# Two-layer hybrid decoder trunk: the second layer's first scale and shift loaded and summed by halves, and ScalarE copies q and k in the first mixer

## The chip, the cores and the metric

The kernel runs as one program on one core of a Trainium2 chip. The metric is the device time of one execution in microseconds (us), from runs of the whole program. Of before there are three runs: 723.83 us is their median, 722.95 the lowest and 725.26 the highest. One further execution was profiled and took 724.93 us.

In what follows PE is TensorE, PEld its weight load, DVE is VectorE, ACT is ScalarE, POOL is GpSimd and SP is SyncE, which issues the DMAs of the weights. L12 is line 12 of the kernel.

## The reference

One sequence of 256 tokens with 1024 features goes through two layers. All is f32; the weights are some 265 MiB and each is used once, so that the program streams them from memory. Cut to what matters:

```python
cond = silu(c)                                  # one row of 1024
for l in range(2):
    mod = cond @ w_mod[l] + b_mod[l]            # w_mod[l]: 1024 x 6144
    sh1, sc1, g1, sh2, sc2, g2 = split(mod, 6)  # six rows of 1024 features
    h = layer_norm_plain(x) * (1 + sc1) + sh1
    q, k, v, p = split(h @ w_in[l], [512, 1024, 1536])
    a = attention(rope(q), rope(k), v)          # 8 heads of 64, causal
    m = pool_mixer(p, w_pool[l], pool_scale[l])
    x = layer_norm_affine(ALPHA * x + g1 * (concat(a, m) @ w_out[l]), ln1_g[l], ln1_b[l])
    h = layer_norm_plain(x) * (1 + sc2) + sh2
    y = grouped_moe(h)                          # 16 experts of 512, 2 per token
    x = layer_norm_affine(ALPHA * x + g2 * y, ln2_g[l], ln2_b[l])
```

The change is about sh1 and sc1 of the second layer (l = 1), which have to be complete before the second layer's h can be built, and about q and k of the first layer.

## The kernel before

**The stream.** All large weights pass through a ring of 1 MB tiles in SBUF, named wr. A Python class `Stream` (L56) holds them in one list, and SP issues their DMAs in that list's order: a tile is issued when the program frees a tile, as long as fewer than the allowed number (20) are live. A tile that is full therefore holds the stream up until PE or DVE has read it. The list for a layer is: the four quarters of w_in for q and k, p, v (two tiles each), the small w_pool, then the rows of w_mod for v = 2, 4, 3 (four tiles each; v counts sh1, sc1, g1, sh2, sc2, g2 as 0 to 5), w_out (four), v = 5 (four), and the eight pairs of experts. One pair is four tiles each of gate, up and down weights. Behind v = 5 of the first layer stand the four tiles of the second layer's v = 1, and behind the first layer's last expert the four of its v = 0; then come the second layer's q and k tiles. The first layer's own v = 0 and 1 are read in quarters of 256 features at the very start, between the q and k tiles.

**The work on them.** A row of mod is cond times 1024 x 1024 weights. PE does it in `mod_mm` (L297): 16 matmuls with cond as a stationary column, in four strips of the PE array that add up in one bank of PSUM. `mod_fin` copies that bank (ACT, L330), transposes it with four matmuls (L335), and DVE reduces it to 8 columns of 128 features and adds the bias (L337, L339). v = 5 ends in a row that is spread over all partitions. For v = 2, 4 and 3 DVE multiplies and adds the weights itself (`mod_dve`: L359 once and L361 seven times a row, one operation per 1024 x 128 weights), and PE closes the partial sums (L372, DVE L373 and L374).

**The mixer.** xn, the normalised x, is transposed by PE (L437, in `enter`), and DVE and ACT write it to hT with scale and shift (L442, L444). Then q and k of both token tiles are multiplied (L455), p (L504), rope is applied by DVE (L740 to L745), q and k are transposed again (L527), and copied to SBUF (L528: q by DVE, k by ACT); the scores follow (L534, L539), DVE's mask and row maximum on them (L554, L555), v (L578), the output (L622) and the norm. Then the router, and the experts: gate and up by L918, down by L960, with the norm of the next mixer at their end (L1104 to L1162).

**Order.** Each engine runs its instructions in the order in which the Python code issues them. `warm(n)` (L283) is a row of n matmuls on constants whose result nobody reads. In the first layer `mod_mm(l + 1, 1)` stands ahead of the norms and the router; in the second layer `warm(7)` stands at about the same place. `mod_fin(l + 1, 1)` is called in the first layer's second expert pair (pair 1 counted from 0).

Of the kernel before, what the change touches and what calls it, by code (L numbers as in the profile page):

```python
# [8 lines left out]
F = mybir.dt.float32  # L9
# [4 lines left out]
OP = mybir.AluOpType  # L14
AX = mybir.AxisListType

D = 1024
# [56 lines left out]
def tile_trunk(ctx, tc, x, c, w_mod, b_mod, w_in, w_pool, pool_scale, w_out, ln1_g, ln1_b,  # L74
# [30 lines left out]
    def add_mod01(h):  # L105

        w = w_mod[0].rearrange("(p k) n -> p k n", k=8)
        for v in (1, 0):
            st.add(("m01", h, v), w[:, :, v * D + h * 256:v * D + (h + 1) * 256])

    def add_qk(l, q):
        st.add(("in", l, "qk", q), w_in[l].rearrange("(k p) n -> p k n", p=128)[:, 2 * q:2 * q + 2, 0:D])

    def add_in(l):
        w = w_in[l].rearrange("(k p) n -> p k n", p=128)
        if l:
            for q in range(4):
                add_qk(l, q)
        for i, nm in ((3, "p"), (2, "v")):
            for q in range(2):  # L120
                st.add(("in", l, nm, q), w[:, 4 * q:4 * q + 4, i * 512:(i + 1) * 512])
# [35 lines left out]
    for l in range(DEPTH):  # L157
        add_in(l)
        st.add(("wp", l), lambda l=l: load_wp(l))
        for v in (2, 4, 3):  # L160
            add_mod(l, v)
        add_out(l)
        add_mod(l, 5)
        if l + 1 < DEPTH:
            add_mod(l + 1, 1)
        for i in range(NPAIR):
            add_pair(l, i)
        if l + 1 < DEPTH:
            add_mod(l + 1, 0)

# [77 lines left out]
    def bias_cols():  # L248
        b = ps()
        bv = b[:, 0:256].rearrange("p (m k r) -> p m k r", m=2, k=8)  # L250
        for k in range(8):
            T.transpose(bv[:, 0, k, 0:NV], brow[0:NV, k * 128:(k + 1) * 128], ident[0:NV, 0:NV])
            T.transpose(bv[:, 1, k, 0:NV], brow[0:NV, k::8], ident[0:NV, 0:NV])
        V.tensor_copy(bcol[:, :, :, 0:NV], bv[:, :, :, 0:NV])
        V.tensor_scalar(bcol[:, 0, :, 1], bcol[:, 0, :, 1], 1.0, None, op0=OP.add)

# [44 lines left out]

    col01 = const.tile([128, 2, 8], F, name="col01")
    colt[0, 0], colt[0, 1] = col01[:, 0], col01[:, 1]

# [14 lines left out]
    def mod01_fin(h, part):  # L319
        b = ps()  # L320
        for k in range(2):
            T.transpose(b[:, k * 128:(k + 1) * 128], part[:, k * 128:(k + 1) * 128], ident)
        o = col01[:, :, 2 * h:2 * h + 2]
        V.reduce_sum(o, b[:, 0:256].rearrange("p (k v o r) -> p v k o r", k=2, v=2, o=2)[:, :, :, :, 0], axis=AX.X)
        V.tensor_add(o, o, bcol[:, 0, 2 * h:2 * h + 2, 0:2].rearrange("p k v -> p v k"))

    def mod_fin(l, v):
# [102 lines left out]

    def enter(l, t, hT, xn):

        for h in range(2):
            b = ps()
            for k in range(4):
                kk = 4 * h + k
                T.transpose(b[:, k * 128:(k + 1) * 128], xn[:, t, kk * 128:(kk + 1) * 128], ident)  # L437
            for k in range(4):
                kk = 4 * h + k
                o, i = hT[:, kk, t * 128:(t + 1) * 128], b[:, k * 128:(k + 1) * 128]  # L440
                if h and t:
                    V.tensor_scalar(o, i, colt[l, 1][:, kk:kk + 1], colt[l, 0][:, kk:kk + 1], op0=OP.mult, op1=OP.add)  # L442
                else:
                    A.activation(o, i, AF.Identity, scale=colt[l, 1][:, kk:kk + 1], bias=colt[l, 0][:, kk:kk + 1])  # L444

    def mixer(l, hT, xn, ready):
        pq = [[ps(), ps()] for _ in range(2)]

        def qk_mm(t, qs=range(4), kks=range(2)):
            for q in qs:  # L450
                w = st.get(("in", l, "qk", q))
# [7 lines left out]

        if l:  # L460
            ready(0)
            qk_mm(0)
            ready(1)
        else:

# [10 lines left out]
        for t in range(2):  # L476
            if t:
                qk_mm(1, range(4) if l else (3,))
            A.activation(qk[:, t, 0:512], pq[t][0], AF.Copy, scale=DH ** -0.5)
# [43 lines left out]
        for t in range(2):  # L523
            for n, dst in ((0, qT), (1, kT)):
                b = ps()
                for cq in range(4):
                    T.transpose(b[:, cq * 128:(cq + 1) * 128], qk[:, t, n * 512 + cq * 128:n * 512 + (cq + 1) * 128], ident)  # L527
                (A.copy if n else V.tensor_copy)(dst[:, :, t * 128:(t + 1) * 128], b.rearrange("p (c s) -> p c s", c=4))  # L528

# [187 lines left out]
        gate = mod_fin(l, 5)  # L717
        if l + 1 < DEPTH:
            mod_mm(l + 1, 1)
        norms_of(1)  # L720
        exps(0)
        if l + 1 == DEPTH:
            warm(7)

# [116 lines left out]
    def experts(l, xh, xl, posm, rest):  # L841
# [230 lines left out]
        for i in range(NPAIR):  # L1072
# [19 lines left out]
            if i == 3:  # L1092
                gather(4)
            if i == 1 and l + 1 < DEPTH:
                mod_fin(l + 1, 1)
            if more:
# [27 lines left out]
    for l in range(DEPTH):  # L1124
# [19 lines left out]
        else:  # L1144
            mod_mm(l, 0)
            warm(3)
            own = []

            def ready(t):
                b = tiny.tile([128, 2, 6], F, name="bn")  # L1150
                if not t:
                    own.append(ends(0))
                for n in range(2):
# [4 lines left out]
                if not t:  # L1158
                    mod_fin(l, 0)
                    warm(8)  # L1160
                    own.append(ends(1))
                V.tensor_scalar(xn[:, t], xt[:, t], mv[:, 0:1], rs, op0=OP.subtract, op1=OP.mult)  # L1162
                enter(l, t, hT, xn)
        xh, xl, mes, gate = mixer(l, hT, xn, ready)
# [48 lines left out]
```

## Time and profile before

| | us |
|---|---|
| median of three runs (lowest, highest) | 723.83 (722.95, 725.26) |
| profiled execution | 724.93 |
| its span, first to last instruction | 723.1 |
| PE busy | 678.9 (94%) |
| DVE busy | 326.8 (45%) |
| ACT busy | 124.8 (17%) |
| DMA queue of SP: bytes, share of the 16 engines | 279.20 MB, 96.1% |

The span is 1.8 us short of the profiled execution's time. PE and the DMA queue are both busy nearly throughout: the page's slices show the DMA share at nine tenths or more except in four slices of the second layer (six or seven tenths), and in the last. By stages, the first mixer, norm and router end at 159.3 us, the first layer's experts run to 363.3, the second mixer, norm and router to 507.1, the second layer's experts to 709.5, and the last norm and the store of the output end the span.

In the rows of a window the engines stand in the order PE, PEld, DVE, ACT, POOL; a granted clock of 1.00 is TensorE's full 2.4 GHz and 0.50 its lower level of 1.2 GHz. In the rows of a timeline a group "x32" is 32 instructions; what stands in square brackets is the idle time of the engine just before the group and what ended it.

### The profile page before, as it was taken

Reading aid. Unit: us, or ns where it says so; the run is one execution under the profiler, and the core shown is the slowest. Engines: PE = TensorE matmul, PEld = TensorE weight load, DVE = VectorE, ACT = ScalarE, POOL = GpSimd, SP = SyncE. Lnnn points to the kernel's source line nnn. Section 1 sums busy time; section 2 is a strip of 40 time slices with the busy share of each in tenths; the row PEclk is TensorE's granted clock in tenths of the full one; section 3 lists DMA queues with packets and bytes.
Section 4 is the critical chain, followed back from the end, with each engine's and each line's share of the span. In section 5 each row is a group of like instructions: output and inputs, shape, how many; then the busy total and the mean of one; then the engine's idle time right before and its main releaser. Section 6 shows DMA issues by size and latency. Waiting matters only on the chain. (4 is left out here: it accounts for less than half of the span.)

```text
span 723.1 us, 8334 instructions
## 1 busy us (share of the span) xinstructions
PE 678.9 (94%) x3213; PEld 316.8 (44%) x3218; DVE 326.8 (45%) x582; ACT 124.8 (17%) x268; POOL 49.7 (7%) x76
## 2 busy tenths in 40 slices
PE   5999899999999999989979999998999999998994
PEld 2447555553333533423324575555333344342331
DVE  4008897662332532413153966666323243241305
ACT  1011432130110210121002035213210011012100
POOL 5001501100000000000010051010000000000002
PEclk9999999999999999999989999999999999999998
DMA  9999999999999999999999999767699999999992
GB/s 307 366 384 409 408 409 420 373 421 392 424 420 420 422 421 421 420 416 418 395 406 392 409 410 406 310 272 301 282 420 422 421 424 419 420 422 418 418 395 77
DMA packets 61729, 280.37 MB, mean 388 GB/s; under 512 B 5008, under 2 KB 14264, under 8 KB 38632
## 3 DMA queue, kind: packets, MB, share of 16 engines
q1 hardware_dynamic: 61040, 279.20, 96.1%
q8 instruction: 30, 0.49, 0.3%
q10 hardware_dynamic: 312, 0.32, 0.1%
q0 software_dynamic: 320, 0.14, 0.1%
q14 instruction: 27, 0.22, 0.1%
HBM read 278.59 MB, written 1.05 MB: 387 GB/s over the span
## 5 line engine op out<-in xcount | busy, mean ns | idle before, releaser
L918 PE MATMUL ps<-wr 128*64 128x512 f32 x1024 | 226.1, 596 | 0.0
L918 PEld LDWEIGHTS ps<-wr 128*64 128x64 f32 x1024 | 73.5, 138 | 147.2 <-issue 142.3
L960 PE MATMUL ps<-wr,s 128*64 128x512 f32 x512 | 113.8, 595 | 3.7 <-DVE s L945 2.9
L960 PEld LDWEIGHTS ps<-wr,s 128*64 128x64 f32 x512 | 35.5, 137 | 72.0 <-issue 63.8
L970 DVE SCALAR_TENSOR_TENSOR s<-ps,gc,gb 128x512 f32<-128x512 f32 x32 | 24.0, 748 | 84.0 <-PE ps L960 84.0
L455 PE MATMUL ps<-wr,hT 128*128 128x512 f32 x128 | 57.0, 597 | 0.4 <-ACT hT L429 0.2
L361 DVE SCALAR_TENSOR_TENSOR wr<-wr,condT 128x1024 f32<-128x1024 f32 x42 | 55.8, 1329 | 2.3 <-DMA wr<-in_w_mod_dram 0.9
L622 PE MATMUL ps<-wr,hT 128*128 128x512 f32 (+1 forms) x160 | 55.7, 507 | 0.1
L389 POOL TENSOR_TENSOR rs<-rs,mhalf 128x1 f32<-128x1 f32 x16 | 13.2, 823 | 554.1 <-DVE rs L388 554.1
L935 DVE TENSOR_TENSOR s<-s,ps 128x512 f32<-128x512 f32 x16 | 11.0, 687 | 86.5 <-PE ps L918 86.5
L973 ACT CAST wr<-s 128x512 fp32r<-128x512 f32 x30 | 18.5, 618 | 164.7 <-PE ps L918 107.7
L974 DVE TENSOR_TENSOR wr<-s,wr 128x512 fp32r<-128x512 f32 x30 | 20.8, 692 | 55.6 <-ACT wr L973 55.6
L622 PEld LDWEIGHTS ps<-wr,hT 128*128 128x128 f32 x160 | 30.2, 190 | 23.8 <-issue 21.5
L455 PEld LDWEIGHTS ps<-wr,hT 128*128 128x128 f32 x128 | 23.6, 190 | 28.9 <-issue 27.1
L984 PE MATMUL ps<-wr,sT 128*128 128x512 f32 x120 | 33.6, 413 | 0.0
L578 PE MATMUL ps<-wr,hT 128*128 128x512 f32 x64 | 28.3, 595 | 0.0
L504 PE MATMUL ps<-hT,wr 128*128 128x256 f32 x128 | 28.1, 380 | 0.0
L984 PEld LDWEIGHTS ps<-wr,sT 128*128 128x128 f32 x120 | 20.9, 189 | 16.3 <-issue 13.0
L933 DVE SCALAR_TENSOR_TENSOR s<-s,ps 128x512 f32<-128x512 f32 x16 | 11.0, 685 | 36.7 <-ACT s L932 36.7
L504 PEld LDWEIGHTS ps<-hT,wr 128*128 128x128 f32 x128 | 24.2, 190 | 4.5 <-issue 1.3
L876 PE MATMUL ps<-s,xn 128*128 128x512 f32 x64 | 25.4, 398 | 0.3 <-DVE s L854 0.3
L996 DVE TENSOR_TENSOR xt<-xt,ps 128x512 f32<-128x512 f32 x40 | 25.2, 683 | 0.5
(240 smaller groups left out, 611.5 us busy)
## 6 DMA issues: line engine op xcount, KB each, us to landing
wr<-in_w_gate_dram SPq DMA_DIRECT2D x64, 1024.0 KB, 19.3
wr<-in_w_up_dram SPq DMA_DIRECT2D x60, 1024.0 KB, 19.3
wr<-in_w_down_dram SPq DMA_DIRECT2D x56, 1024.0 KB, 19.5
wr<-in_w_mod_dram SPq DMA_DIRECT2D x48, 1024.0 KB, 15.1
wr<-in_w_in_dram SPq DMA_DIRECT2D x16, 1024.0 KB, 15.1
wr<-in_w_out_dram SPq DMA_DIRECT2D x8, 1024.0 KB, 18.7
wr<-in_w_down_dram SPq DMA_DIRECT2D x12, 512.0 KB, 11.1
wr<-in_w_up_dram SPq DMA_DIRECT2D x8, 512.0 KB, 17.4
```

Source lines behind the costliest of these rows:

```text
L361: V.scalar_tensor_tensor(acc, w[:, kk], condT[:, k, 0:1], acc, op0=OP.mult, op1=OP.add)
L455: T.matmul(pq[t][n], hT[:, k, t * 128:(t + 1) * 128], w[:, kk, n * 512:(n + 1) * 512], start=(k == 0), stop=(k == 7))
L504: T.matmul(pp[g // 2][:, (g % 2) * 256:(g % 2) * 256 + 256], w[:, kk, g * 128:(g + 1) * 128], hT[:, k, :], start=(k == 0 and g % 2 == 0), ...
L578: T.matmul(pv[t], hT[:, k, t * 128:(t + 1) * 128], w[:, kk, :], start=(k == 0), stop=(k == 7))
L622: T.matmul(py[t][-1][:, 0:c1 - c0], catT[:, k, t * 128:(t + 1) * 128], w[:, kk, n * 512 + c0:n * 512 + c1], start=(q == 2 and kk == 0), st ...
L876: T.matmul(b, xs[:, t, k * 128:(k + 1) * 128], SX[i][t], start=(n == 0), stop=(n == 3))
L918: T.matmul(bs[nm][64 * j:64 * j + 64, :], XE[i][k // 4][:, k % 4, c0:c0 + 64], st.get((nm, l, 2 * i + j, q))[:, k - k0, :], start=(k == 0) ...
L960: T.matmul(bo[n][64 * j:64 * j + 64, :], AT[i][:, k, 64 * j:64 * j + 64], st.get(("d", l, 2 * i + j, q))[:, k - k0, (n - n0) * 512:(n - n0 ...
L970: V.scalar_tensor_tensor(o, bo[n], GC[i], g2[:, c0], op0=OP.mult, op1=OP.mult)
L974: V.tensor_sub(ol[:, c0], o, oh[:, c0].bitcast(F))
L984: T.matmul(b, STt[i][:, t * 128:(t + 1) * 128], o[:, n * 512:(n + 1) * 512], start=(start and j == 0), stop=(stop and j == 1), skip_group_ ...
L996: V.tensor_add(b if i == NPAIR - 3 else xt[:, t, c0], xt[:, t, c0], b)
```

## The change

The first layer's stream loses the four tiles of v = 1 ahead of the experts. Behind the first layer's last expert, v = 1 and v = 0 of the second layer are now read by halves of 512 features: four tiles of 128 x 4 x 512 for features 0 to 511 (v = 1 and 0, two halves of the rows each), two of q and k's quarters, four tiles for features 512 to 1023, and the other two quarters. Each half is summed by PE in `mod1`: 16 matmuls, one copy by ACT, and closed in `mod1_fin` by four transposes, one reduction for scale and shift together and one addition of the biases. The 1 that is added to the scale is now in the bias columns (L252 to L255 before).

The second mixer's opening is written out anew: transposes of token tile 0's first half, q and k of token tile 0 from the first two quarters, the second half's `mod1`, then token tile 1, and so on. The normalised xn is written in two halves of 512. In the first layer `warm(7)` now stands where `mod_mm(l + 1, 1)` was, as in the second. In the first mixer ACT makes all four copies of L528 (now L573), of which DVE made two.

In the lines below h is the half, v the row of mod, q the quarter or the half of the rows.

```diff
+    def add_mod1(h):
+        w = w_mod[1].rearrange("(p k) n -> p k n", k=8)
+        for v in (1, 0):
+            for q in range(2):
+                st.add(("m1", h, v, q), w[:, 4 * q:4 * q + 4, v * D + h * 512:v * D + (h + 1) * 512])
     def add_qk(l, q):
...
         w = w_in[l].rearrange("(k p) n -> p k n", p=128)
-        if l:
-            for q in range(4):
-                add_qk(l, q)
         for i, nm in ((3, "p"), (2, "v")):
...
         add_mod(l, 5)
-        if l + 1 < DEPTH:
-            add_mod(l + 1, 1)
         for i in range(NPAIR):
...
         if l + 1 < DEPTH:
-            add_mod(l + 1, 0)
+            for q in range(4):
+                if q % 2 == 0:
+                    add_mod1(q // 2)
+                add_qk(l + 1, q)
...
         V.tensor_copy(bcol[:, :, :, 0:NV], bv[:, :, :, 0:NV])
-        V.tensor_scalar(bcol[:, 0, :, 1], bcol[:, 0, :, 1], 1.0, None, op0=OP.add)
+        V.tensor_scalar(bcol[:, 0, :, 1:8:6], bcol[:, 0, :, 1:8:6], 1.0, None, op0=OP.add)
...
         V.tensor_add(o, o, bcol[:, 0, 2 * h:2 * h + 2, 0:2].rearrange("p k v -> p v k"))
+    def mod1(h):
+        acc = ps()
+        for k in range(8):
+            for v in range(2):
+                j = 2 * v + k % 2
+                T.matmul(acc[32 * j:32 * j + 32, :], condT[:, k, :], st.get(("m1", h, v, k // 4))[:, k % 4, :],
+                         start=(k < 2), stop=(k > 5))
+            if k % 4 == 3:
+                for v in range(2):
+                    st.free(("m1", h, v, k // 4))
+        part = s2()
+        A.copy(part, acc)
+        return part
+    def mod1_fin(h, part):
+        b = ps()
+        for k in range(4):
+            T.transpose(b[:, k * 128:(k + 1) * 128], part[:, k * 128:(k + 1) * 128], ident)
+        o = col01[:, 1, :, 4 * h:4 * h + 4]
+        V.reduce_sum(o, b.rearrange("p (k v o r) -> p v k o r", k=4, v=2, o=2)[:, :, :, :, 0], axis=AX.X)
+        V.tensor_add(o, o, bcol[:, 0, 4 * h:4 * h + 4, 6:8].rearrange("p k v -> p v k"))
...
-    def enter(l, t, hT, xn):
-        for h in range(2):
-            b = ps()
-            for k in range(4):
-                kk = 4 * h + k
-                T.transpose(b[:, k * 128:(k + 1) * 128], xn[:, t, kk * 128:(kk + 1) * 128], ident)
+    def enter(l, t, h, hT, xn):
+        b = ps()
+        for k in range(4):
+            kk = 4 * h + k
+            T.transpose(b[:, k * 128:(k + 1) * 128], xn[:, t, kk * 128:(kk + 1) * 128], ident)
+        def fin():
             for k in range(4):
...
                     A.activation(o, i, AF.Identity, scale=colt[l, 1][:, kk:kk + 1], bias=colt[l, 0][:, kk:kk + 1])
+        return fin
     def mixer(l, hT, xn, ready):
-        pq = [[ps(), ps()] for _ in range(2)]
+        pq = [[], []]
         def qk_mm(t, qs=range(4), kks=range(2)):
+            if not pq[t]:
+                pq[t] += ps(), ps()
             for q in qs:
...
         if l:
             ready(0)
-            qk_mm(0)
+            enter(l, 0, 0, hT, xn)()
+            qk_mm(0, (0, 1))
+            part = mod1(1)
             ready(1)
+            enter(l, 1, 0, hT, xn)()
+            mod1_fin(1, part)
+            fins = [enter(l, 0, 1, hT, xn)]
+            qk_mm(1, (0, 1))
+            fins.append(enter(l, 1, 1, hT, xn))
+            for fin in fins:
+                fin()
+            qk_mm(0, (2, 3))
         else:
...
             if t:
-                qk_mm(1, range(4) if l else (3,))
+                qk_mm(1, (2, 3) if l else (3,))
             A.activation(qk[:, t, 0:512], pq[t][0], AF.Copy, scale=DH ** -0.5)
...
                     T.transpose(b[:, cq * 128:(cq + 1) * 128], qk[:, t, n * 512 + cq * 128:n * 512 + (cq + 1) * 128], ident)
-                (A.copy if n else V.tensor_copy)(dst[:, :, t * 128:(t + 1) * 128], b.rearrange("p (c s) -> p c s", c=4))
+                (A.copy if n or not l else V.tensor_copy)(dst[:, :, t * 128:(t + 1) * 128], b.rearrange("p (c s) -> p c s", c=4))
...
         gate = mod_fin(l, 5)
-        if l + 1 < DEPTH:
-            mod_mm(l + 1, 1)
         norms_of(1)
         exps(0)
-        if l + 1 == DEPTH:
-            warm(7)
+        warm(7)
...
                 gather(4)
-            if i == 1 and l + 1 < DEPTH:
-                mod_fin(l + 1, 1)
             if more:
...
         else:
-            mod_mm(l, 0)
+            part0 = mod1(0)
             warm(3)
...
                 b = tiny.tile([128, 2, 6], F, name="bn")
-                if not t:
-                    own.append(ends(0))
+                own.append(ends(t))
                 for n in range(2):
...
                 if not t:
-                    mod_fin(l, 0)
+                    mod1_fin(0, part0)
                     warm(8)
-                    own.append(ends(1))
-                V.tensor_scalar(xn[:, t], xt[:, t], mv[:, 0:1], rs, op0=OP.subtract, op1=OP.mult)
-                enter(l, t, hT, xn)
+                for n in range(2):
+                    V.tensor_scalar(xn[:, t, n * 512:(n + 1) * 512], xt[:, t, n * 512:(n + 1) * 512],
+                                    mv[:, 0:1], rs, op0=OP.subtract, op1=OP.mult)
         xh, xl, mes, gate = mixer(l, hT, xn, ready)
```

The order of the instructions at three places follows. First SP's DMAs ahead of the first layer's experts, before and after (mod is w_mod; a row is a run of DMAs of one shape):

```order
L146 DMA wp<-in_w_pool_dram 128x4x128
L56 DMA wr<-in_w_mod_dram 128x2x1024 x12
L56 DMA wr<-in_w_out_dram 128x2x1024 x4
L56 DMA wr<-in_w_mod_dram 128x2x1024 x8
L56 DMA wr<-in_w_gate_dram 128x2048 x4
```

```order
L150 DMA wp<-in_w_pool_dram 128x4x128
L56 DMA wr<-in_w_mod_dram 128x2x1024 x12
L56 DMA wr<-in_w_out_dram 128x2x1024 x4
L56 DMA wr<-in_w_mod_dram 128x2x1024 x4
L56 DMA wr<-in_w_gate_dram 128x2048 x4
```

The twelve tiles for v = 2, 4, 3 and w_out stay; of the eight tiles for v = 5 and the second layer's v = 1, four remain.

Next SP's DMAs from the first layer's last down weights on, before and after:

```order
L56 DMA wr<-in_w_down_dram 128x2x512 x6
L56 DMA wr<-in_w_down_dram 128x512 x4
L56 DMA wr<-in_w_mod_dram 128x2x1024 x4
L56 DMA wr<-in_w_in_dram 128x2x1024 x4
L56 DMA wr<-in_w_in_dram 128x4x512 x4
L146 DMA wp<-in_w_pool_dram 128x4x128
```

```order
L56 DMA wr<-in_w_down_dram 128x2x512 x6
L56 DMA wr<-in_w_down_dram 128x512 x4
L56 DMA wr<-in_w_mod_dram 128x4x512 x4
L56 DMA wr<-in_w_in_dram 128x2x1024 x2
L56 DMA wr<-in_w_mod_dram 128x4x512 x4
L56 DMA wr<-in_w_in_dram 128x2x1024 x2
L56 DMA wr<-in_w_in_dram 128x4x512 x4
L150 DMA wp<-in_w_pool_dram 128x4x128
```

Four tiles of 2 rows x 1024 have become two groups of four tiles of 4 rows x 512, the second one between the second and the third quarter of q and k.

Last, PE at the opening of the second mixer, from the last row of `warm` to p, before and after (col names are left out by the view; L437 and L466 are the transposes into hT, L455 and L489 q and k, L340 `mod1`, L352 its transposes, L504 and L549 p):

```order
L283 MATMUL ps<-ones 128x512
L437 MATMUL ps<-ident,xn 128x128 x8
L455 MATMUL ps<-wr,hT 128x512 x16
L437 MATMUL ps<-ident,xn 128x128 x8
L455 MATMUL ps<-wr,hT 128x512 x16
L504 MATMUL ps<-hT,wr 128x256 x32
```

```order
L288 MATMUL ps<-ones 128x512
L466 MATMUL ps<-ident,xn 128x128 x4
L489 MATMUL ps<-wr,hT 128x512 x8
L340 MATMUL ps<-wr,condT 32x512 x16
L466 MATMUL ps<-ident,xn 128x128 x4
L352 MATMUL ps<-ident,s_5813 128x128 x4
L466 MATMUL ps<-ident,xn 128x128 x4
L489 MATMUL ps<-wr,hT 128x512 x8
L466 MATMUL ps<-ident,xn 128x128 x4
L489 MATMUL ps<-wr,hT 128x512 x16
L549 MATMUL ps<-hT,wr 128x256 x32
```

Before, PE ran both token tiles' q and k one after the other, each after eight transposes. Now the second half's `mod1` and its transposes stand after the first eight matmuls of q and k, and all that follows stands behind them.

## Rows read from the trace of the kernel before

**Rows 1.** Both layers' experts: length, busy us (instructions) by engine, clock, DMA share, GB/s

```profile
159.34:363.32 203.98, 198.07 (x914) 77.28 (x913) 64.85 (x116) 25.74 (x42) 0.00 (x0) 0.99 1.01 415
507.08:709.47 202.39, 197.18 (x910) 76.81 (x909) 64.49 (x114) 25.26 (x41) 0.00 (x0) 1.00 0.97 400
```

**Rows 2.** The page's 40 slices: TensorE's granted clock in tenths, GB/s of the DMAs

```profile
PEclk9999999999999999999989999999999999999998
...
GB/s 307 366 384 409 408 409 420 373 421 392 424 420 420 422 421 421 420 416 418 395 406 392 409 410 406 310 272 301 282 420 422 421 424 419 420 422 418 418 395 77
```

**Rows 3.** Waits of SP, window 140 to 170: us in total, times, longest

```profile
SPq L56 <- PE ps L918: 20.2, 3, 15.0
```

**Rows 4.** Waits of SP, window 484 to 520

```profile
SPq L56 <- PE ps L918: 22.6, 3, 17.4
```

**Rows 5.** DMA issued at 163.0 to 163.2: KB, us to landing

```profile
wr<-in_w_up_dram SPq DMA_DIRECT2D x1, 1024.0 KB, 5.8
```

**Rows 6.** DMA issued at 510.7 to 510.9

```profile
wr<-in_w_up_dram SPq DMA_DIRECT2D x1, 1024.0 KB, 5.0
```

**Rows 7.** Last expert DMA of the first layer, issued at 353.4

```profile
wr<-in_w_down_dram SPq DMA_DIRECT2D x1, 256.0 KB, 8.0
```

**Rows 8.** Timeline of DVE in the first mixer: start, us, operation, idle before and releaser

```profile
63.05 10.82 DVE L361 SCALAR_TENSOR_TENSOR wr<-wr,condT 128x1024 f32<-128x1024 f32 x7
73.79 1.27 DVE L528 COPY wr<-ps 128x512 f32<-128x512 f32 x2
76.77 0.70 DVE L554 TENSOR_TENSOR ps<-ps,mask 128x512 f32<-128x512 f32 x1 [1.70 <-PE ps L534]
...
88.54 9.21 DVE L361 SCALAR_TENSOR_TENSOR wr<-wr,condT 128x1024 f32<-128x1024 f32 x7
```

**Rows 9.** Timeline of ACT in the first mixer

```profile
69.42 1.07 ACT L513 COPY wr<-ps 128x512 f32<-128x512 f32 x2 [14.45 <-PE ps L504]
```

**Rows 10.** Timeline of DVE ahead of the first layer's experts

```profile
140.54 1.23 DVE L646 TENSOR_SCALAR wr<-xt,mv,rs 128x1024 f32<-128x1024 f32 x1 [0.73 <-POOL rs L389]
```

**Rows 11.** Timeline of PE: first mixer, router, pair 1, boundary, second mixer

```profile
74.62 2.08 PE L534 MATMUL ps<-wr 64*128 64x128 f32 x16 [3.48 <-DVE wr L528]
...
135.54 7.05 PE L297 MATMUL ps<-wr,condT 128*32 128x512 f32 x64
...
200.35 0.66 PE L335 MATMUL ps<-ident,s 128*128 128x128 f32 x4 [1.22 <-ACT s L330]
...
372.74 1.93 PE L297 MATMUL ps<-wr,condT 128*32 128x512 f32 x8 [2.49 <-DMA wr<-in_w_mod_dram]
...
380.43 1.98 PE L455 MATMUL ps<-wr,hT 128*128 128x512 f32 x4
...
409.25 13.98 PE L504 MATMUL ps<-hT,wr 128*128 128x256 f32 x64
...
428.36 1.16 PE L534 MATMUL ps<-wr 64*128 64x128 f32 x16 [0.35 <-DVE wr L528]
...
488.04 1.67 PE L283 MATMUL ps<-ones 128*128 128x512 bf16 x7
```

**Rows 12.** Windows: the loads of p and v, then those of w_mod in the second layer

```profile
382.91:393.79 10.88, 10.88 (x26) 4.75 (x25) 1.78 (x4) 0.00 (x0) 0.55 (x1) 1.00 1.05 386
394.65:415.10 20.45, 20.34 (x66) 11.75 (x65) 17.96 (x18) 3.65 (x8) 0.15 (x1) 1.00 1.03 409
```

**Rows 13.** Last DMAs for v = 4 of the second layer, issued at 396.3

```profile
wr<-in_w_mod_dram SPq DMA_DIRECT2D x2, 1024.0 KB, 18.7
```

**Rows 14.** Timeline of DVE in the second mixer

```profile
410.09 7.89 DVE L361 SCALAR_TENSOR_TENSOR wr<-wr,condT 128x1024 f32<-128x1024 f32 x6 [0.37 <-DMA wr<-in_w_mod_dram]
...
420.37 0.29 DVE L745 TENSOR_TENSOR xn<-s 128x128 f32<-128x128 f32 x1
425.86 1.29 DVE L373 TENSOR_REDUCE col<-ps 128x4 f32<-128x512 f32 x2 [5.20 <-PE ps L372]
```

**Rows 15.** A window with the clock at its lower level

```profile
74.61:78.03 3.42, 3.41 (x24) 3.26 (x26) 1.69 (x3) 0.00 (x0) 3.18 (x6) 0.50 1.04 413
```

More of the change, by code (lines that the diff above doesn't have):

```diff
@@ L300, in mod_mm @@
         macc[l, v] = acc
-    col01 = const.tile([128, 2, 8], F, name="col01")
-    colt[0, 0], colt[0, 1] = col01[:, 0], col01[:, 1]
+    col01 = const.tile([128, DEPTH, 2, 8], F, name="col01")
+    for l in range(DEPTH):
+        for v in range(2):
+            colt[l, v] = col01[:, l, v]
     def mod01(h):
@@ L322, in mod01_fin @@
             T.transpose(b[:, k * 128:(k + 1) * 128], part[:, k * 128:(k + 1) * 128], ident)
-        o = col01[:, :, 2 * h:2 * h + 2]
+        o = col01[:, 0, :, 2 * h:2 * h + 2]
         V.reduce_sum(o, b[:, 0:256].rearrange("p (k v o r) -> p v k o r", k=2, v=2, o=2)[:, :, :, :, 0], axis=AX.X)
         V.tensor_add(o, o, bcol[:, 0, 2 * h:2 * h + 2, 0:2].rearrange("p k v -> p v k"))
+    def mod1(h):
[6 more added lines that the diff above has]
+            if k % 4 == 3:
+                for v in range(2):
+                    st.free(("m1", h, v, k // 4))
[9 more added lines that the diff above has]
+        V.tensor_add(o, o, bcol[:, 0, 4 * h:4 * h + 4, 6:8].rearrange("p k v -> p v k"))
     def mod_fin(l, v):
```

## The prediction

> **What bounds the kernel now.** I read the windows by stage first. In both layers' experts PE and the DMA queue are full together: PE is busy 198.1 of 204.0 us and 197.2 of 202.4 us, and the DMAs move 415 and 400 GB/s [rows 1]. So the end follows the start of the second layer's experts by a fixed 202.4 us and a tail, and what the change gains in the first layer counts only if it is still there at 507.1.
>
> Next the waits of SP and single DMAs, to see which of the two sets the length of the first layer's experts. When these start, 19 expert tiles are in the ring, and SP stands 15.0 us at the next one until PE frees a gate tile [rows 3]; in the second layer the same wait is 17.4 us [rows 4]. This 20th tile lands 5.8 us after its issue at 163.1, thus at 168.9, some 0.8 us later behind its issue than in the second layer (5.0), where the queue had run dry [rows 5, 6]. The layer's last expert piece lands at 353.4 + 8.0 = 361.4 [rows 7]. Between lie 192.5 us. The layer has 96 expert tiles (16 experts, three matrices of 2 MB); 96 - 19 = 77, so a tile takes 2.50 us, which is 420 GB/s, as the slices there show, nearly all 420 to 424 [rows 2]: the queue has no pause. The first layer's experts are therefore bound by DMA from the 20th tile on, and by nothing else that the change touches.
>
> Then the timelines, for what stands ahead of the 20th tile and behind the last piece.
>
> **First mixer: ACT copies q.** DVE's seven L361 end at 63.05 + 10.82 = 73.87, and only then can it copy q (1.27 us for two); the mask waits further for the scores and starts at 76.77 [rows 8]. ACT is free at 69.42 + 1.07 = 70.49, and makes a copy of that size in 0.54 [rows 9]; four end at about 72.7, so PE's scores, now at 74.62 after 3.48 idle [rows 11], can start near 71.5 and the mask right at 73.87. DVE gains 76.77 - 73.87 = 2.9. Its next seven L361 (88.54, 9.21, without a pause) [rows 8] come that much earlier, and the mixer waits for them: -2.9. Bounds: nothing, if another engine holds the mixer, and -3.5, PE's whole idle time.
>
> **Ahead of the experts: `mod_mm` out, `warm(7)` in.** PE's 64 L297 run from 135.54 to 142.59 [rows 11], half of them this row's (3.5 us), while DVE has the normalised rows at 140.54 + 1.23 = 141.77 [rows 10]. PE was late by 0.8; without the 32 it is at 139.1, with `warm` (1.67 us, row at 488.04) [rows 11] at 140.7, and DVE is last: -0.8. The experts start 3.7 earlier.
>
> **The ring takes the head start.** Four tiles (10 us of stream) fewer stand ahead of the experts. But the ring holds no more than before: the queue runs dry at the 19th tile and waits for PE, as it does in the second layer. So the 20th tile is issued 3.7 earlier and lands 5.0 instead of 5.8 after it: 4.5 earlier, and so does the last expert piece, at 356.9. The 4 MB that the stream had carried early are now behind it. From the other side: if the queue did not run dry, they would come 10 us earlier.
>
> **Pair 1: `mod_fin` out.** PE's pause of 1.22 and 0.66 of transposes at 200.35 [rows 11] go. Nothing comes of it where DMA sets the end; I count 0 (bound -1.9).
>
> **Behind the last expert.** Before, v = 0 (4 tiles) is complete at about 372.7 and q and k start at 380.43, 7.7 later [rows 11]. Now the first half's four tiles have runs of 2 KB per partition row, as p and v have; those load at 386 GB/s, 2.72 us a tile, and the rows of w_mod with 4 KB runs at 409, 2.56 [rows 12]. I take 2.72 (bounds 2.50, a tile of the experts, and 2.87, by the 366 GB/s of the second slice [rows 2], in which rows of w_mod with 1 KB runs are loaded). The half lands at 356.9 + 10.9 = 367.8. Of the 7.7 I take off up to 1.4 (four transposes instead of eight, half a norm): q and k at 374 to 375.5. Half of a token tile's q and k takes a quarter of 409.25 - 380.43 = 28.8 [rows 11], 7.2; the second half lands at 367.8 + 5.1 + 10.9 = 383.8, so PE waits 1 to 2.5 us. One us of `mod1`, about 2 for copy, transposes and hT, and 21.6 of q and k put p at 408 to 410, where it was: PE keeps nothing of the 4.5.
>
> **The second mixer's v = 4.** This is the step that decides. Before, the last tile of v = 4 lands at 396.3 + 18.7 = 415.0 [rows 13], 53.6 behind the last expert piece. Now there are eight tiles for four: 53.6 - 4 x 2.56 + 8 x 2.72 = 65.1, so it lands at 356.9 + 65.1 = 422.0, 7.0 later. Behind it DVE has two more L361 and rope, and then idles 5.20 until PE is through with p and the transposes (425.86) [rows 14]. 7.0 - 5.2 = 1.8: DVE is late now, by that much, and the copies, the scores and the whole second half of the mixer follow. From there to 507.1 the DMAs fall to 272 to 310 GB/s [rows 2], so they don't bound it, and the experts start 1.8 later.
>
> **Sum.** -2.9 (first mixer), -0.8 (`mod_mm`) and -0.8 (the dry queue) make -4.5 at the last expert piece. The stream behind it is 8 x 2.72 - 4 x 2.56 = 11.5 longer, and DVE had 5.2 to spare: -4.5 + 11.5 - 5.2 = +1.8. Against the profiled execution, 724.93, that is 726.7; the median of the runs lies 1.1 lower, at 723.83, so I forecast 725.6.
>
> **A rule on short runs.** The loads with 2 KB runs go at 386 GB/s, against 409 for 4 KB [rows 12]. The Trainium skill, "DMA: Bandwidth & Descriptors", Specifications, gives 512 B as the least transfer for line rate; by it the eight tiles would go at the experts' speed. That would be a rival: in rows, eight tiles at 2.50, 8 x 0.22 = 1.8 less, no change, 723.8. The row of p and v speaks against it; for it only that four tiles are a short sample.
>
> **The rivals.** *The gain stays (faster).* If the mixer opens so much better that DVE's v = 4 is not last, or the stream keeps its lead, PE's path counts: 3.7 and 1.9 from pair 1 less about 1.6 for the new wait, -4.0, thus 719.8. For it speaks the PE work taken out ahead of the experts; against it the 15.0 us at a full ring [rows 3]. *The clock falls (slower).* PE's wait of 3.48 at 74.62 was followed by 3.42 us at 0.50 [rows 15], in which the 16 L534 took 2.08 instead of 1.16 [rows 11]. Now PE has new waits: 1 to 2.5 us for the second half near 383, and about 1.5 ahead of the scores near 429, where it had 0.35 [rows 11]. If the clock falls there, half of 3.42 is lost on PE: +1.7 once, 727.3, and +3.4 twice, 729. It decides where a new wait is nearer to 3.48 than to 0.35, which left the later L534 at full speed. The Trainium skill, "TensorE: Matmul & The Clock Gate", Part 1, has the clock fall after idling, and this trace agrees with its 0.50 behind the wait. *The first mixer gains nothing (slower).* If DVE's later work, or PE's, holds the first mixer where it was, the 2.9 are missing at v = 4: +4.7, 728.5.
>
> **How the numbers follow.** Forecast 0.44 (724 to 727); the short runs are free 0.12 (723.8); the gain stays 0.22 (719.8 to 721.5); the clock falls 0.14 (727.3 to 729); no gain in the first mixer 0.08 (728.5). About 0.3% (2.2 us) is what a measurement of this kernel can tell from no change: faster is below 721.7, slower above 726.0. Faster takes the third case, 0.22. Slower takes the last two and a third of the forecast's, 0.14 + 0.08 + 0.15 = 0.37. Same has the rest, 0.41. The range from 720.3 to 728.2 leaves out about half of the third case and half of the last two.
>
> **What would show it.** In the profile after: the first mixer's mask right behind L391 near 73.9 and no low clock there; the experts' start near 155.6; the DMAs dry for some 10 us ahead of it; the first layer's last expert landing near 356.9; p starting within 2 us of 409; DVE with no idle time between rope and the reduction (L403), which starts near 427.7; the second layer's experts near 508.9. I am wrong if v = 4 lands before 420, if the queue does not run dry ahead of the first layer's experts, or if something between the reduction and the router takes up the delay.

## The result: 1.6% slower, and the profile after

The changed kernel takes 735.88 us (median of 4 runs, 734.74 to 737.44) against 724.24 of before (now four runs): a ratio of 1.0163 (95% interval 1.0135 to 1.0192), 11.6 us more where I had forecast 1.8. The profiled execution is the slowest of the four, 737.44, with a span of 735.6.

Up to the first layer's last expert things went as drawn, only smaller. The slices of the DMAs' rate first:

```profile
GB/s 306 365 385 409 409 414 420 387 172 422 421 420 419 420 420 418 419 414 410 387 395 390 409 409 409 312 257 368 216 419 421 419 419 421 418 419 416 417 396 80
```

The ninth slice, ahead of the experts, fell from 421 in [rows 2] to 172 GB/s: the queue ran dry, from the landing of the 19th expert tile at 154.9 to the issue of the next at 162.1. SP's wait there is now as long as the second layer's was [rows 3, 4]:

```profile
SPq L56 <- PE ps L960: 22.6, 3, 17.4
```

Of the DMAs, the 20th expert tile (issued at 162.1), the last expert piece (351.96) and the last two tiles of v = 4 (the later one at 406.3), with KB and us to landing:

```profile
wr<-in_w_up_dram SPq DMA_DIRECT2D x1, 1024.0 KB, 5.2
...
wr<-in_w_down_dram SPq DMA_DIRECT2D x1, 256.0 KB, 8.1
...
wr<-in_w_mod_dram SPq DMA_DIRECT2D x2, 1024.0 KB, 18.8
```

The last expert piece lands at 360.0, 1.4 earlier than before and not 4.5 [rows 7]; v = 4 lands at 425.1, 10.0 later than before [rows 13]. Between them are 65.1 us, the number that I had worked out: the tiles' rate was right, the head start was not.

DVE in the first mixer (start, us, operation), as in [rows 8]:

```profile
63.91 10.82 DVE L391 SCALAR_TENSOR_TENSOR wr<-wr,condT 128x1024 f32<-128x1024 f32 x7
74.66 0.69 DVE L599 TENSOR_TENSOR ps<-ps,mask 128x512 f32<-128x512 f32 x1
...
87.07 9.21 DVE L391 SCALAR_TENSOR_TENSOR wr<-wr,condT 128x1024 f32<-128x1024 f32 x7
```

ACT's copies let the mask follow L391 without a pause, at 74.66. But this execution had begun 0.9 us late (p at 56.17, before at 55.31; the thirteen profiles of this document have it anywhere from 55.24 to 57.68), and the next seven L391 start only 1.5 earlier than before.

PE: first the second mixer's v in the kernel before, which [rows 11] don't show; then, after, from the first mixer's transposes of v = 4 to the second mixer's v:

```profile
431.19 7.13 PE L578 MATMUL ps<-wr,hT 128*128 128x512 f32 x16
```

```profile
96.43 1.45 PE L402 MATMUL ps<-ident,wr 128*128 128x128 f32 x8 [2.38 <-DVE wr L391]
97.81 1.98 PE L646 MATMUL ps<-wr 128*64 128x128 f32 x16
...
412.43 13.98 PE L549 MATMUL ps<-hT,wr 128*128 128x256 f32 x64
...
433.32 1.94 PE L572 MATMUL ps<-ident,xn 128*128 128x128 f32 x8 [3.88 <-DVE xn L787]
...
438.25 2.08 PE L579 MATMUL ps<-wr 64*128 64x128 f32 x16
...
442.79 7.13 PE L623 MATMUL ps<-wr,hT 128*128 128x512 f32 x16
```

PE now waits 2.38 for v = 4 at 96.43, and there is the low clock behind it; p of the second mixer starts at 412.43, 3.2 later than before; and ahead of the transposes of q and k PE waits 3.88. The low clock in two windows:

```profile
97.07:100.48 3.41, 3.41 (x23) 2.26 (x22) 3.19 (x5) 0.59 (x1) 1.06 (x1) 0.50 1.03 412
431.58:441.82 10.24, 7.40 (x40) 6.37 (x42) 8.18 (x18) 1.17 (x2) 8.04 (x15) 0.50 1.02 410
```

DVE in the second mixer, from v = 4 through rope to the reduction, which answers to [rows 14]:

```profile
420.07 7.89 DVE L391 SCALAR_TENSOR_TENSOR wr<-wr,condT 128x1024 f32<-128x1024 f32 x6 [0.32 <-DMA wr<-in_w_mod_dram]
427.88 2.08 DVE L782 TENSOR_TENSOR s<-xn,cs 128x128 f32<-128x128 f32 x1
429.88 0.28 DVE L783 TENSOR_TENSOR s<-xn,cs 128x128 f32<-128x128 f32 x1
430.08 1.61 DVE L784 TENSOR_TENSOR s<-xn,cs 128x128 f32<-128x128 f32 x1
431.62 0.28 DVE L785 TENSOR_TENSOR s<-xn,cs 128x128 f32<-128x128 f32 x1
431.93 1.05 DVE L786 TENSOR_TENSOR xn<-s 128x128 f32<-128x128 f32 x1
432.90 0.28 DVE L787 TENSOR_TENSOR xn<-s 128x128 f32<-128x128 f32 x1
433.10 0.82 DVE L782 TENSOR_TENSOR s<-xn,cs 128x128 f32<-128x128 f32 x1
433.85 0.30 DVE L783 TENSOR_TENSOR s<-xn,cs 128x128 f32<-128x128 f32 x1
434.07 0.47 DVE L784 TENSOR_TENSOR s<-xn,cs 128x128 f32<-128x128 f32 x1
434.46 0.28 DVE L785 TENSOR_TENSOR s<-xn,cs 128x128 f32<-128x128 f32 x1
434.77 0.70 DVE L786 TENSOR_TENSOR xn<-s 128x128 f32<-128x128 f32 x1
435.40 0.30 DVE L787 TENSOR_TENSOR xn<-s 128x128 f32<-128x128 f32 x1
435.62 1.27 DVE L403 TENSOR_REDUCE col<-ps 128x4 f32<-128x512 f32 x2
```

Here is what I had not seen at all. Rope starts 10.0 late, by as much as v = 4 lands late, and then its twelve operations, 0.28 us each before, take 7.8 us together instead of 2.8 (427.88 to 435.70, before 417.90 to 420.66): six of them take 0.47 to 2.08. POOL in the same stretch does the pooling of p. Its first operation before, then its operations after:

```profile
423.99 1.99 POOL L749 TENSOR_TENSOR wr<-wr 128x1084 f32<-128x1084 f32 x1 [13.91 <-ACT wr L513]
```

```profile
427.16 2.65 POOL L791 TENSOR_TENSOR wr<-wr 128x1084 f32<-128x1084 f32 x1 [8.64 <-DMA wr<-in_w_mod_dram]
429.89 1.66 POOL L792 TENSOR_TENSOR wr<-wr 128x807 f32<-128x807 f32 x1
431.63 1.20 POOL L793 TENSOR_TENSOR wr<-wr 128x530 f32<-128x530 f32 x1
432.91 0.86 POOL L794 TENSOR_TENSOR wr<-wr 128x256 f32<-128x256 f32 x1
```

Each slow operation of DVE ends just behind one of POOL's: 427.88 + 2.08 = 429.96 behind 427.16 + 2.65 = 429.81; 431.69 behind 431.55; 432.98 behind 432.83; 433.92 behind 433.77. The last two, at 434.07 and 434.77, end in the same way behind two shorter operations of POOL's. Before, rope was over at 420.7 and POOL began at 424. The reduction behind it, L403, reads PSUM and takes 1.27 beside POOL, before 1.29.

In the profiled executions the second layer's experts start 11.6 late, at 518.7 against 507.1. These are: 1.4 saved up to the last expert piece; 11.4 of stream added; 5.2 of DVE's slack used up; 5.0 for rope beside POOL; and about 1.8 from the reduction (9.8 late) to v on PE (442.79 against 431.19, 11.6 late), with the clock at 0.50. -1.4 + 11.4 - 5.2 + 5.0 + 1.8 = 11.6. The two spans are 12.5 apart; the other 0.9 arises behind that start. That the medians of the runs are 11.6 apart too is chance.

### The profile page after: what moved, and what is told of

Its sections match the earlier page's. It is cut to its first block, busy times and chain, and to the rows that moved or that the text cites. A ratio compares the mean times of both kernels' runs of the same rounds, so it can differ in the third digit from the quotient of the medians.

```text
span 735.6 us, 8361 instructions
## 1 busy us (share of the span) xinstructions
PE 688.3 (94%) x3225; PEld 321.8 (44%) x3225; DVE 331.2 (45%) x582; ACT 126.2 (17%) x270; POOL 50.9 (7%) x76
## 5 line engine op out<-in xcount | busy, mean ns | idle before, releaser
L489 PE MATMUL ps<-wr,hT 128*128 128x512 f32 x128 | 57.1, 596 | 0.5 <-ACT hT L475 0.5
L391 DVE SCALAR_TENSOR_TENSOR wr<-wr,condT 128x1024 f32<-128x1024 f32 x42 | 55.8, 1329 | 2.3 <-DMA wr<-in_w_mod_dram 0.9
L489 PEld LDWEIGHTS ps<-wr,hT 128*128 128x128 f32 x128 | 23.5, 190 | 28.3 <-issue 26.8
L549 PE MATMUL ps<-hT,wr 128*128 128x256 f32 x128 | 28.1, 380 | 0.0
L549 PEld LDWEIGHTS ps<-hT,wr 128*128 128x128 f32 x128 | 24.2, 190 | 4.5 <-issue 1.0
## 6 DMA issues: line engine op xcount, KB each, us to landing
wr<-in_w_down_dram SPq DMA_DIRECT2D x12, 512.0 KB, 11.6
```

Source lines behind the costliest of these rows:

```text
L391: V.scalar_tensor_tensor(acc, w[:, kk], condT[:, k, 0:1], acc, op0=OP.mult, op1=OP.add)
L489: T.matmul(pq[t][n], hT[:, k, t * 128:(t + 1) * 128], w[:, kk, n * 512:(n + 1) * 512], start=(k == 0), stop=(k == 7))
L549: T.matmul(pp[g // 2][:, (g % 2) * 256:(g % 2) * 256 + 256], w[:, kk, g * 128:(g + 1) * 128], hT[:, k, :], start=(k == 0 and g % 2 == 0), ...
```

## The experiments

Each ratio is to the runs of the kernel before that stand beside that run on record. Their medians differ (723.0 to 724.5 us), so rows are compared by their ratios. Microseconds won or lost are worked out from these ratios at 724 us, and positions from the one profiled execution of each run.

| run | median us (runs) | ratio to before (95% interval) |
|---|---|---|
| the change | 735.9 (4) | 1.0163 (1.0135, 1.0192) |
| e1: POOL waits for rope | 730.2 (4) | 1.0087 (1.0053, 1.0120) |
| e2: PE's wait ahead of q, k filled | 735.1 (4) | 1.0165 (1.0136, 1.0193) |
| e4: change, DVE copies q | 738.8 (4) | 1.0209 (1.0181, 1.0238) |
| e7: change, v behind v = 4 | 728.0 (10) | 1.0059 (1.0041, 1.0078) |
| e8: e7 and filled wait in first mixer | 727.6 (12) | 1.0042 (1.0026, 1.0058) |
| e3: before, DVE delayed 6.6 us | 731.9 (4) | 1.0113 (1.0085, 1.0142) |
| e11: e3, POOL waits for rope | 727.8 (10) | 1.0050 (1.0030, 1.0070) |
| e9: before, the move alone | 733.2 (4) | 1.0119 (1.0088, 1.0151) |
| e5: before, ACT copies alone | 721.8 (12) | 0.9971 (0.9954, 0.9987) |
| e6: e5 and filled wait | 721.1 (12) | 0.9953 (0.9933, 0.9974) |
| e10: e6 and filled wait at the boundary | 721.8 (12) | 0.9966 (0.9951, 0.9982) |

**e1: POOL held until rope is through** (from the changed kernel).

```diff
+        if l:
+            P.tensor_copy(tiny.tile([128, 1], F, name="hold", bufs=1), qk[:, 1, 8:9])
         pr = pool(pz, SA, SB)
```

> The changed kernel, with one small copy on POOL that reads the last of rope's output ahead of the second mixer's pooling, so that POOL starts when DVE is through with rope. Theory (POOL's pooling, running beside it, slows rope from 2.8 to 7.7 us): rope takes 2.8 us, the reduction behind it starts near 430.7 instead of 435.6, PE waits about 1.5 us there, and the time is 5 to 7 us under the changed kernel's, 729 to 731. Rival (rope is slow for another reason, or POOL's lateness costs as much elsewhere): rope stays at 7 us, or the time stays at 735 to 737.

DVE, the first and last of rope's operations and what follows:

```profile
428.20 0.28 DVE L784 TENSOR_TENSOR s<-xn,cs 128x128 f32<-128x128 f32 x1
...
430.67 0.28 DVE L789 TENSOR_TENSOR xn<-s 128x128 f32<-128x128 f32 x1
430.87 1.28 DVE L403 TENSOR_REDUCE col<-ps 128x4 f32<-128x512 f32 x2
432.19 1.23 DVE L404 SCALAR_TENSOR_TENSOR col<-col,bcol 128x8 f32<-128x8 f32 x1
```

and POOL's first:

```profile
431.40 1.99 POOL L793 TENSOR_TENSOR wr<-wr 128x1084 f32<-128x1084 f32 x1
```

Rope takes 2.75 us again, and by the ratios 5.5 of the 11.8 us are gone. No work was left out, POOL only starts later. What stays, 6.3 us, has three parts in the profile: the reduction 5.0 late, L404 now beside POOL itself (1.23 instead of 0.43), and PE's wait of 1.30 for the copies with the low clock behind it. (That execution began 2.4 us later than before's, p at 57.68, so its 5.0 can't be set against the 6.3 of the runs.)

**e3 and e11: the same delay put into the kernel before.** Five operations on the finished sums of v = 4 hold DVE up ahead of rope, values unchanged; e11 adds the line of e1.

```diff
             mod_dve(l, 4, acc[4])
+            for _ in range(5):
+                V.scalar_tensor_tensor(acc[4], acc[4], 1.0, acc[4], op0=OP.mult, op1=OP.max)
         rope(qk)
```

> The kernel before, with five more DVE operations of 1.3 us (6.6 us) on the partial sums of v = 4 ahead of rope in the second mixer; the stream is as before. Theory (DVE has 5.2 us to spare, and past about 3 us it meets POOL's pooling, which starts at 424.0): rope starts at 424.5 and takes 7 to 8 us, the reduction starts at 432, the clock falls behind PE's wait, and the time is 6 to 8.5 us over before, 730 to 732.5. Rival (a delay ahead of rope costs only what goes beyond the slack): 6.6 - 5.2 = 1.4 us more, 725.5.

> The kernel before with the same five DVE operations ahead of rope in the second mixer as in the run with a late v = 4, and POOL's pooling held until rope is through. Theory (of the cost of that delay only 6.6 - 5.2 = 1.4 to 3 us are the delay itself, the rest was the two engines side by side and the clock): rope takes 2.8 us, the reduction starts near 429, time 2 to 4.5 us over before. Rival (the delay costs the same whatever POOL does): 7.5 to 9 us over before, as there.

DVE in e3: the five operations, rope's first, the reduction:

```profile
418.13 7.93 DVE L489 SCALAR_TENSOR_TENSOR wr<-wr 128x1024 f32<-128x1024 f32 x5
425.99 1.61 DVE L742 TENSOR_TENSOR s<-xn,cs 128x128 f32<-128x128 f32 x1
...
432.10 1.27 DVE L373 TENSOR_REDUCE col<-ps 128x4 f32<-128x512 f32 x2
```

and in e11:

```profile
418.68 6.26 DVE L489 SCALAR_TENSOR_TENSOR wr<-wr 128x1024 f32<-128x1024 f32 x5
424.86 0.28 DVE L744 TENSOR_TENSOR s<-xn,cs 128x128 f32<-128x128 f32 x1
...
427.53 1.28 DVE L373 TENSOR_REDUCE col<-ps 128x4 f32<-128x512 f32 x2
```

Without a byte moved in the stream, a delay of 6.3 us made the kernel before 8.2 us slower, 1.13%, and 3.6 us with POOL held. From the first of the five to the reduction it is 13.97 us in the one and 8.85 in the other: 5.1 us for the two engines side by side, on the added operations (7.93 against 6.26) as well as on rope. The rival, by which a delay costs only what goes beyond the slack of 5.2, is refuted by e3. With POOL held the cost, 3.6, is still more than the 1.1 that this rival would have (6.3 - 5.2); POOL then runs beside L374 and the clock falls behind it (0.50 near 433), and what each of these costs was not tried.

**e2: PE's wait ahead of the transposes of q and k filled** (from the changed kernel).

```diff
         if l:
             fin_shift()
+            warm(18)
```

> The changed kernel, with 18 matmuls on constants in PE's order ahead of the second mixer's transposes of q and k, where PE waits 3.9 us for rope. Theory (the wait makes the clock fall for the 10 us behind it, and that alone costs 1.8 us): granted clock 1.00 from 430 to 445, rope still 7.7 us, 734 (1.8 less). Rival (the low clock is hidden behind DVE): same time as the changed kernel, 735 to 737.

The window over that stretch has the clock at 1.00, with rope as slow as in the change:

```profile
430.00:445.00 15.00, 12.57 (x72) 7.47 (x71) 13.95 (x26) 5.90 (x26) 9.00 (x16) 1.00 1.02 408
```

In this profile v follows the reduction by 5.3 us (435.04 to 440.30), as in the kernel before, instead of 7.2, so there the 1.8 are gone. But the time is 0.8 us less by the medians and the same by the ratios. What the low clock cost there is thus not settled by the runs; the 1.8 us of the profiles are the most that can be said for it.

**e7: v behind v = 4 in the stream** (from the changed kernel): a change of order alone.

```diff
-    def add_in(l):
+    def add_in(l, part=((3, "p"), (2, "v"))):
...
-        for i, nm in ((3, "p"), (2, "v")):
+        for i, nm in part:
...
-        add_in(l)
+        add_in(l, ((3, "p"),) if l else ((3, "p"), (2, "v")))
         st.add(("wp", l), lambda l=l: load_wp(l))
         for v in (2, 4, 3):
             add_mod(l, v)
+            if l and v == 4:
+                add_in(l, ((2, "v"),))
```

> The changed kernel, with the second layer's two tiles of v (w_in) moved in the stream behind the four tiles of v = 4. Nothing is added or taken away. Theory (the landing of v = 4 sets rope, rope then meets POOL's pooling, and PE's wait lowers the clock): v = 4 lands 5.4 us earlier, near 419.7, rope runs at 422.5 to 425.3 in 2.8 us ahead of POOL, PE's p (ending at 426.2) is the bound, and the time is 3 to 4 us over before, 727, that is 9 less than the changed kernel. Rival (the stream's order is hidden and the second mixer's opening on PE costs the time): 732 or more.

DVE there, from v = 4 to the reduction:

```profile
412.29 7.89 DVE L393 SCALAR_TENSOR_TENSOR wr<-wr,condT 128x1024 f32<-128x1024 f32 x6 [0.35 <-DMA wr<-in_w_mod_dram]
420.10 0.29 DVE L784 TENSOR_TENSOR s<-xn,cs 128x128 f32<-128x128 f32 x1
...
422.57 0.28 DVE L789 TENSOR_TENSOR xn<-s 128x128 f32<-128x128 f32 x1
426.66 1.29 DVE L405 TENSOR_REDUCE col<-ps 128x4 f32<-128x512 f32 x2 [3.81 <-PE ps L404]
```

Rope is at full speed and over before POOL starts (424.8), DVE idles 3.81 again, and by the ratios 7.5 us of the 11.8 are back. So it was the landing of v = 4 that carried these 7.5. What stays, 4.3, was not taken apart; in the profile the reduction waits for PE again, and PE's p starts 52.4 us behind the last expert piece, as in the change, against 47.8 before. **e8** adds ten matmuls (`warm(10)`, first layer only) between the two calls in `fin_shift`:

> The same, with ten matmuls on constants where PE waits for v = 4 in the first mixer. Theory: clock 1.00 from 94 to 160, everything from there to the first layer's last expert piece 1.2 to 1.5 us earlier, and the end too: 1.5 to 2.5 us over before, 725.5. Rival (the clock there is hidden): as the run before it.

1.0042 against 1.0059: the intervals overlap, the 1.2 to 1.5 us are not shown. In the profile of e7 the clock had not fallen in the first mixer, so that in this execution there was nothing to win.

**e9: the move alone, from the kernel before.** The second layer's v = 1 goes behind the last expert in whole rows, its `mod_mm` and `mod_fin` to the opening of the second mixer, and `warm(7)` takes the place of `mod_mm` in the first layer.

```diff
-        if l + 1 < DEPTH:
-            add_mod(l + 1, 1)
...
         if l + 1 < DEPTH:
+            add_mod(l + 1, 1)
             add_mod(l + 1, 0)
...
```

> The kernel before, with only the move: the second layer's v = 1 is loaded behind the last expert ahead of v = 0, both in whole rows of 1024 as before, and summed and closed there; warm(7) stands in the first layer in the place of its matmuls; DVE copies q in the first mixer; q and k wait for all eight tiles. Theory (the four tiles cost what they take in the stream, since the ring was full ahead of the experts anyway): last expert piece 0.8 to 1.6 us earlier, v = 4 lands 8.7 to 9.5 us later than before, near 424; PE's p ends 8 to 9 us later than before, and the time is 8 to 10 us over before, 733. Rival (the halves and the order at the opening are what costs): within 3 us of before.

```profile
418.90 7.89 DVE L360 SCALAR_TENSOR_TENSOR wr<-wr,condT 128x1024 f32<-128x1024 f32 x6 [0.33 <-DMA wr<-in_w_mod_dram]
426.70 0.28 DVE L736 TENSOR_TENSOR s<-xn,cs 128x128 f32<-128x128 f32 x1
...
434.54 1.29 DVE L372 TENSOR_REDUCE col<-ps 128x4 f32<-128x512 f32 x2 [5.08 <-PE ps L371]
```

The move by itself costs 8.6 us. Here q and k wait for all eight tiles, so PE is last (DVE idles 5.08 ahead of the reduction, which is 8.7 late), POOL comes after rope, and there is no collision. The halves of the change do bring p forward (412.43 against 417.93 here), but that made the landing of v = 4 the last thing to arrive, and POOL, which follows p, met rope.

**e4: DVE copies q in the first mixer** (the changed kernel without that part).

> The changed kernel with DVE copying q in the first mixer, as before; all else is the change. Theory (what ACT's copies gain is lost again in PE's wait for v = 4 at 96 us and the low clock behind it): experts of the first layer start within 0.7 us of the changed kernel's 158.4, and the time is the same, 735 to 737. Rival (the copies do gain 2.9 us, as I had it): the experts start at 161 and the time is 738 to 739.

My theory, the same time, fell: the medians are 738.8 without the copies and 735.9 with them, 2.9 apart, and 3.3 by the ratios, though the two intervals just touch. In the profiles the first layer's experts start at 159.7 without and 158.4 with them, 1.3 apart. Counted from the start of p it is 103.7 us without, 102.2 in the change and 100.7 in e7, where the clock had not fallen behind PE's wait for v = 4; so how much of the 2.9 gets through may differ from execution to execution, which these runs don't show.

**e5, e6 and e10: what the first mixer's part gives to the kernel before.** e5 is one line of the change, e6 adds `warm(10)` ahead of v = 4's transposes in the first layer, e10 also fills PE's waits for the last two tiles of v = 0 with 5 and 11 matmuls.

```diff
-                (A.copy if n else V.tensor_copy)(dst[:, :, t * 128:(t + 1) * 128], ...)
+                (A.copy if n or not l else V.tensor_copy)(dst[:, :, t * 128:(t + 1) * 128], ...)
...
             mod_dve_fin(l, 2, acc[2])
+            if not l:
+                warm(10)
             mod_dve_fin(l, 4, acc[4])
```

> The kernel before, with only the four copies of q and k in the first mixer given to ACT. Theory (DVE gains 2.9 us, PE then waits 2.4 us for v = 4 and runs the next 3.4 us at the low clock, which gives half of it back; and the stream, full up to the first layer's experts, keeps most of the rest): out projection of the first layer 1.4 us earlier, the last expert piece 0.8 to 1.4 us earlier, time 0.5 to 1.5 us under before. Rival (the 2.9 us reach the end): 2.9 us under before.

> The same, with ten matmuls on constants where PE waits for v = 4 in the first mixer (about 94 to 96 us). Theory (the wait lets the clock fall; filled, it doesn't): granted clock 1.00 from 94 to 160, the experts start 1.4 us earlier than in the run with ACT's copies alone; the stream lets at most another 1 us of it through, time 1 to 2.5 us under before. Rival (the fall there costs nothing): as the run without the ten matmuls.

> The kernel before with ACT's copies and the ten matmuls in the first mixer, and now 5 and 11 matmuls on constants also where PE waits for the last two tiles of v = 0 behind the last expert. Theory (this wait lets the clock fall for up to 6.8 us ahead of q and k, on PE's path): granted clock 1.00 from 365 to 380 in every execution, q and k 1 to 2 us earlier, time 1 to 2 us under the run without them, 719.5 to 720.5. Rival (DVE's norm of the first token tile is the bound there): the same time, 721.

ACT's copies alone make the kernel before 2.1 us faster (0.9 to 3.3), between the theory's 0.5 to 1.5 and the rival's 2.9; the interval takes in parts of both. The fall that the theory counted on did not come in e5's profile (the last lines of this document). PE in e6, where e5 has its wait of 2.37:

```profile
94.26 2.32 PE L283 MATMUL ps<-ones 128*128 128x512 bf16 x10
96.80 1.14 PE L372 MATMUL ps<-ident,wr 128*128 128x128 f32 x8 [0.22 <-DVE wr L361]
```

e6 is 3.4 us faster than before (1.9 to 4.9), and beats both kernels; whether the ten matmuls have a share in it is not shown, since the intervals of e5 and e6 overlap. e10 adds nothing that the runs show: in the profile of e6 the clock had not fallen at the boundary between the layers, so in that execution there was nothing to fill.

## Why the prediction was wrong

**What bounds the kernel; the ring; the stream behind the last expert: right.** The queue ran dry as drawn, the fixed length of the second layer's experts held to 0.9 us, and v = 4 landed 65.1 us behind the last expert piece. That this fits to the tenth is luck, as the rate of the new tiles was open from 2.50 to 2.87 us. One count was off: behind the landing of the 20th expert tile stand 76 tiles and not 77, which makes 2.53 us a tile. The reading stands, since the DMAs moved 418 GB/s over that whole stretch, and its length was 192.6 us before and 192.8 after. The rival by which 2 KB runs load at the full rate is out, and so is the one in which the gain stays.

**The first mixer and `mod_mm`: right in kind, too large.** I had 3.7 us at the start of the experts; the profile has 0.9, and this execution's late beginning hides another 0.9. DVE's gain of 2.9 shrank to 2.3 on its way to v = 4's transposes (from the mask to the seven L391 it took 12.4 instead of 11.8), and PE, by then waiting 2.38, ran on at half speed and gave 1.6 of it back. The other profiles bear this out. From the start of p to the experts' start the kernel before takes 104.0 us (55.31 to 159.34); the change takes 102.2 and e2 102.3, both with the clock fallen behind that wait; e1, e7 and e8, in which it had not fallen, take 100.7. Without the fall 3.3 of the 3.7 are there. I had named PE's wait and its clock at other places, and had not looked for the next wait behind the one that I removed. At the last expert piece 3.1 us are missing in all, some 2.5 of them by the late beginning (0.9) and the clock (1.6). The opening of the second mixer on PE took as long as I had it, 52.4 us from that piece to p where I had 51 to 53, so p was 3.2 late for the missing head start alone, outside the 2 us that I had set.

**The second mixer's v = 4: the step that failed.** It said that DVE is late by 7.0 - 5.2 "by that much, and the copies, the scores and the whole second half of the mixer follow". It took rope at its old length. Late by 10, rope runs beside POOL's pooling and takes 5.0 more (e1, e3, e11 and e7 each show it by another edit). The sign was right here, the price was not. The rows had a hint: seven L361 take 10.82 at 63.05 and 9.21 at 88.54 [rows 8], the same operations on the same shapes, and I did not ask what else ran in the first stretch. It is POOL's pooling, whose first operation runs from 70.63 to 72.79 in the kernel before: six of the seven take 1.28, and the one that starts at 70.97 takes 2.90.

**The clock: a rival that came true on top.** I gave it 0.14 as something in place of the forecast. It came with it, since a late rope is what makes PE wait: 3.88 us, and the low clock for 10.2. Its price, 1.8, is from the profiles alone; the runs of e2 don't confirm it.

The terms: 3.1 (head) + 5.0 (rope) + 1.8 (clock) = 9.9 us beyond the forecast's 1.8.

## What to carry to other kernels

A stage that is moved in time gets new neighbours: before its old durations are used in a sum, look who else runs at the new time on the memory that it uses, and whether two rows of one operation with different lengths already tell. Four tiles taken from a stretch where the ring is full buy little, and cost their whole length where the queue never rests. Behind each wait that is removed, look for the next one on the same engine: here PE's new wait of 2.38 us was followed by half the clock in two of five profiles.

## What the runs showed of the hardware

DVE and POOL, working on SBUF at once, wait for each other by whole operations: an operation of DVE's of 0.28 us took 2.08, and ended 0.15 us after POOL's, and that one of POOL's took 2.65 instead of 1.99. DVE's reads of PSUM beside POOL were not slowed (1.27). The Trainium skill, "SBUF — State Buffer", "SBUF: two separate sides", says that these two engines share one pair of ports under an exclusive lock, held for a whole instruction; the rows agree.

A PE wait of the same length does not always bring the clock down. At v = 4's transposes in the first mixer it was 2.35 to 2.39 us in five profiles; behind it the clock was at 0.50 for 3.4 us in two (the change and e2), and at full speed in e1, e5 and e7. In e5:

```profile
97.04:101.00 3.96, 3.96 (x31) 2.81 (x32) 3.16 (x5) 0.58 (x1) 1.06 (x1) 1.00 1.03 411
```
